# Where the split weights of a hybrid decoder block start in SBUF: six slots of 512-byte multiples

## The chip, the cores and the metric

The kernel runs on one core of one Trainium2 chip. The metric is the device time of one execution in microseconds (us); smaller is better. A difference of about 0.2% is what repeated timing of this kernel can tell from no change.

## The reference

One layer of a decoder block over 512 tokens of 2048 channels, in float32. Nearly all of its work is in dense products with weight matrices:

```python
mod = c_act @ w_ada[l] + b_ada[l]                      # 6 x 2048 modulation values
h = rmsnorm(x, norm_mix_g[l]) * (1.0 + sc_m) + sh_m
proj = h @ w_in[l]                                     # nine parts: conv, HGRN2, two gates
y_a = (a_b * causal_depthwise_conv(a_c * a_x, conv_w[l])) @ w_conv_out[l]
o = hgrn2_chunked(qh, kh, vh, log_f)                   # chunks of 64 tokens, 8 heads
y_b = o.reshape(b, s, D_HGRN_V).astype(x.dtype) @ w_hgrn_out[l]
merged = jax.nn.sigmoid(gate_a) * y_a + jax.nn.sigmoid(gate_b) * y_b
x = x + gt_m * (merged @ w_o[l])
h2 = rmsnorm(x, norm_ffn_g[l]) * (1.0 + sc_f) + sh_f
ff = (jax.nn.silu(h2 @ w_ffn_gate[l]) * (h2 @ w_ffn_up[l])) @ w_ffn_down[l]
return rmsnorm(x + gt_f * ff, norm_final_g)
```

## The kernel before, in words

Activations stand channel-major: 128 channels by 512 tokens. A product keeps float32 accuracy by splitting both operands into a high part, rounded to the reduced type `fp32r`, and a low part, the rest. It then needs three matmuls for each pair of blocks: high weights with high activations, high weights with low activations, low weights with high activations. `mm3` (lines 233 to 235), `v_block` (lines 351 to 353) and `m3` (lines 629 to 631) write out these three. Every matmul comes with its own load of a 128 by 128 block of weights, which the profile lists as engine PEld and which runs ahead of the matmul it belongs to.

Weights come by DMA as raw float32 tiles in the order of use. ScalarE casts a raw tile into `hi`, VectorE subtracts to get `lo` (lines 166 and 167 in `w_prep`; 674 to 684 in `quad_s` and `quad_c`; 1085 and 1086 in `u_prep`, where the tiles are called `uh` and `ul`). Each of the two names has a ring of three buffers, so weights are prepared up to two tiles ahead. `w_tile` makes a tile of the wanted size plus 32 elements, and starts the weights either at the beginning of the tile or, with `half`, 16 elements (64 bytes) into it.

Which weights take `half`:

- Without it: weights used with 512 columns of activations at once. These are the projections of the first and third stage (`proj`, `panel`, lines 233 to 235) and the down projection of the FFN (`down`, kind "D", lines 629 to 631). Also without it: the weights of `v_block`, where the activations are the loaded block and the weights are what streams through, 256 columns at a time.
- With it: weights used with 256 columns. These are the Strassen and plain passes of the gates and of the FFN (kinds "S" and "C", lines 629 to 631) and the token halves of the output projection.
- Kind "H" (eight tiles of the first FFN pass) is not in the ring: these weights stay for a second use in tiles of the pool `sactb`.

In time the program runs as follows. From 0 to about 157 us are the first norm, the modulation of the first norm on VectorE, and the first panels of `w_in`. Up to about 773 us come the rest of `w_in` and the HGRN2 core, the latter spread as background work. Up to about 1055 us are the gates (256 columns). Up to about 1400 us come the output projections of the two branches and `w_o`, beside which VectorE computes the other modulation values from 92 tiles of `w_ada` (line 311). The rest is the FFN, where the passes of 256 columns alternate with `down` (512 columns), and a tail.

The tiles are placed one behind the other in SBUF. In the first rings (pool `wts`) a tile takes 1056 elements, 4224 bytes, which is 8 times 512 plus 128; in the FFN's rings (pool `wts2`) it takes 928 elements, 3712 bytes, 7 times 512 plus 128. The first slot starts at a multiple of 512 bytes (117760 and 39936). So the six slots start 0, 128, 256 bytes (the three of `hi`) and 384, 0, 128 bytes (the three of `lo`) past a multiple of 512. A block of 128 weights is 512 bytes long, so every block in a tile has the offset of its tile. In use the slots follow each other as **A** (hi 0, lo 384), **B** (hi 256, lo 128), **C** (hi 128, lo 0), A, and so on.

Of the kernel before, what the change touches and what calls it, by code (L numbers as in the profile page):

```python
# [9 lines left out]
F32R = mybir.dt.float32r  # L10
# [4 lines left out]
P = 128  # L15
T = 512
D = 2048
# [25 lines left out]
WFULL = 5  # L43
HCB = 5
WOFF = 16

COL_C = 0
COL_B = 16
# [14 lines left out]
def hybrid_block_kernel(ctx: ExitStack, tc: tile.TileContext, xt, cols, crow, wam, war, wst, win, wco, who, wo, wgt, wg, wu, wd,  # L63
# [4 lines left out]
    def nm(s):  # L68
        cnt[0] += 1
        return f"{s}{cnt[0]}"  # L70
# [13 lines left out]
    wp = s1.enter_context(tc.tile_pool(name="wts", bufs=3, reuse_waits="tile"))  # L84
# [47 lines left out]
    def flat(t):  # L132
        return t.rearrange("p a b -> p (a b)")

    wlist = []
    wstate = {"dma": 0, "prep": 0, "use": 0, "raw": {}, "hl": {}, "half": ()}

    def w_tile(pool, shape, tag, name, half):
        a, b = shape[1:]
        t = pool.tile([P, a * b + 32], F32R, tag=tag, name=nm(name))  # L140
        o = WOFF if half else 0
        return t[:, o:o + a * b].rearrange("p (a b) -> p a b", b=b)

    def w_pair(shape, half=False):
        return [w_tile(wp, shape, t, t, half) for t in ("hi", "lo")]

    def w_dma():
        i = wstate["dma"]
# [8 lines left out]
    def w_prep():  # L157
        i = wstate["prep"]
        if i >= len(wlist):
            return  # L160
        while wstate["dma"] <= i:
            w_dma()
        raw = wstate["raw"].pop(i)
        hi, lo = w_pair((P, 4, 256), i in wstate["half"])
        nw = wlist[i].shape[-1]
        S.copy(flat(hi)[:, 0:nw], raw[:, 0:nw])  # L166
        V.tensor_tensor(flat(lo)[:, 0:nw], raw[:, 0:nw], flat(hi)[:, 0:nw].bitcast(F32), op=ALU.subtract)  # L167
        wstate["hl"][i] = (hi, lo)
        wstate["prep"] = i + 1

    def next_w(look=LOOK):
        i = wstate["use"]
        while wstate["prep"] <= min(i + look, len(wlist) - 1):
            w_prep()
        while wstate["dma"] <= min(i + look + 1, len(wlist) - 1):
            w_dma()
        wstate["use"] = i + 1
        return wstate["hl"].pop(i)
# [198 lines left out]
    for n in range(KC):  # L377
        g = n // 4
        w = [flat(t)[:, 0:512 if g else 768].rearrange("p (a b) -> p a b", b=256) for t in next_w(1)]
# [293 lines left out]
    def quad_s(sm, raw, hi, lo):  # L673
        S.copy(hi[:, 0:3, :], raw[:, 1:4, :])  # L674
        V.tensor_tensor(sm[:, 0:2, :], raw[:, 1:3, :], raw[:, 0:1, :].to_broadcast([P, 2, P]), op=ALU.subtract)
        V.tensor_tensor(sm[:, 2, :], sm[:, 1, :], raw[:, 1, :], op=ALU.add)
        V.tensor_tensor(sm[:, 3, :], raw[:, 3, :], sm[:, 2, :], op=ALU.subtract)  # L677
        S.copy(hi[:, 3:7, :], sm)  # L678
        V.tensor_tensor(lo[:, 0:3, :], raw[:, 1:4, :], hi[:, 0:3, :].bitcast(F32), op=ALU.subtract)
        V.tensor_tensor(lo[:, 3:7, :], sm, hi[:, 3:7, :].bitcast(F32), op=ALU.subtract)  # L680
# [85 lines left out]
    def g_prep():  # L766
        i = gs["prep"]
        while gs["dma"] <= i:
            g_dma()
        _, _, u, strassen = glist[i]  # L770
        raw = gs["raw"].pop(i)[:, u, :, :]
        hi, lo = w_pair((P, 8, P), True)
        if strassen:
            quad_s(gs["sm"](), raw, hi, lo)
        else:
            quad_c(raw, hi, lo)
        gs["hl"][i] = (hi, lo)
        gs["prep"] = i + 1
# [191 lines left out]
    torder = [(j, 0) for j in range(TU)] + [(j, 1) for j in range(TU)] + [(j, u) for j in range(TU, 8) for u in range(2)]  # L970
    ulist.extend((wd[j, 10], u, "D" if i < TU else "T") for i, (j, u) in enumerate(torder))
    kept = []
    us = {"dma": 0, "prep": 0, "use": 0, "raw": {}, "hl": {}, "pool": None, "after": ()}

    def u_dma():
        i = us["dma"]
        src = ulist[i][0] if i < tail0 else wd[(i - tail0) // 2, 10]
        raw = wr2.tile([P, 2, 4, P], F32, tag="raw", name=nm("ur"))
        nc.sync.dma_start(raw, src.rearrange("p (u b n) -> p u b n", u=2, b=4))
        if i < tail0:  # L980
            us["raw"][i] = us["raw"][i + 1] = raw
        else:
            for u in range(2):
                us["raw"][tail0 + torder.index(((i - tail0) // 2, u))] = raw
        us["dma"] = i + 2
# [77 lines left out]
    def u_prep():  # L1063
        i = us["prep"]
        while i not in us["raw"]:
            u_dma()
        _, u, kind = ulist[i]
        raw = us["raw"].pop(i)[:, u, :, :]
        pool = us["pool"] if kind == "T" else wp2
        shp = [P, 4, P] if kind == "T" else [P, 7, P]  # L1070
        if kind == "H":
            k = len(kept)
            t = sb[k // 2][k % 2]
            hi, lo = (t[:, 1 + 2 * b:3 + 2 * b, :].rearrange("p a (c n) -> p (a c) n", n=P) for b in range(2))
            kept.append((hi, lo))
        else:
            hi = w_tile(pool, shp, "hi", "uh", kind != "D")
            lo = w_tile(pool, shp, "lo", "ul", kind != "D")
        if kind == "S":
            quad_s(wp2.tile([P, 4, P], F32, tag="sm", name=nm("us"), bufs=2), raw, hi, lo)  # L1080
        else:
            with ExitStack() as order:
                for ins in us["after"] if i >= len(ulist) - 12 else ():
                    order.enter_context(tc.issue_after(ins.ins))
                S.copy(hi[:, 0:4, :], raw)  # L1085
                V.tensor_tensor(lo[:, 0:4, :], raw, hi[:, 0:4, :].bitcast(F32), op=ALU.subtract)  # L1086
        us["hl"][i] = (hi, lo)
        us["prep"] = i + 1

    def u_ahead(n=ULOOK):  # L1090
        i = us["use"]
        for k in range(i, min(i + n + 1, len(ulist))):
            if ulist[k][2] == "T" and us["pool"] is None:
                break
            if us["prep"] <= k:
                u_prep()
        while us["dma"] <= min(i + n + 3, len(ulist) - 2):
            u_dma()
# [206 lines left out]
    for tok in HALF:  # L1305
        outs = []
        for j in range(8):
# [12 lines left out]
            for e in range(2):  # L1320
                n = 2 * j + e
# [82 lines left out]
```

## Time and profile before

| | |
|---|---|
| median of 3 runs | 2822.83 us (2821.8 to 2823.86) |
| the profiled execution | 2818.55 us, span in the trace 2816.8 us |
| mean granted TensorE clock | 0.991 |
| VectorE, ScalarE busy | 2217.8 us (79%), 1100.1 us (39%) |
| DMA traffic | 414.23 MB, 147 GB/s on average |

In the rows that follow, a group of instructions is given as line, engine, operation, output and inputs by the program's names, partitions by elements, count, busy time in us, mean duration of one in ns, and what its engine waited for ahead of it. The recorded duration of a matmul is longer than the distance between the starts of two of them, because they are pipelined. The offsets of the weights are those of the section above; the trace names the tiles but not their addresses.

### The profile page before, as it was taken

What the parts mean: (1) busy time and instruction counts of PE and PEld (TensorE: products, weight loads), DVE (VectorE), ACT (ScalarE), POOL (GpSimd) and SP (SyncE); (2) the same over time, 40 slices, a digit from 0 to 9 for tenths busy, and PEclk for the clock granted to TensorE, in tenths of its full rate; (3) what the DMA queues carried; (4) which work ended last, traced back from release to release, by engine and by line L of the source; (5) the groups of instructions that cost most, each with busy time, mean ns of one, the idle gap of its engine ahead of it and who ended that gap; (6) DMA issues with size and microseconds to landing.
All of it is one profiled execution on the core that took longest, in us unless ns stands there. A gap on an engine that the chain in (4) does not pass through costs nothing.

```text
span 2816.8 us, 46688 instructions
## 1 busy us (share of the span) xinstructions
PE 2741.5 (97%) x18524; PEld 2461.4 (87%) x18524; DVE 2217.8 (79%) x4326; ACT 1100.1 (39%) x1723; POOL 1.3 (0%) x7
## 2 busy tenths in 40 slices
PE   5999999999999999899999999999999999999997
PEld 3788888888799997787899899998989989898997
DVE  7998963836799996786789787796968879687786
ACT  4333422323245552222375343343434334343445
POOL 0000000000000000000000000000000000000000
PEclk8999999999999999999999999999999999999999
DMA  9865632322233348898744333333333333333333
GB/s 351 302 215 187 207 100 83 97 91 90 76 101 118 124 148 298 294 315 287 239 143 127 100 112 101 109 106 98 113 99 112 99 104 113 98 113 98 105 106 105
DMA packets 117616, 414.23 MB, mean 147 GB/s; under 512 B 12818, under 2 KB 17170, under 8 KB 117396
## 3 DMA queue, kind: packets, MB, share of 16 engines
q1 hardware_dynamic: 116244, 407.04, 43.9%
q10 hardware_dynamic: 1152, 4.19, 0.4%
q8 instruction: 145, 2.38, 0.4%
q14 instruction: 75, 0.61, 0.1%
HBM read 398.59 MB, written 12.59 MB: 146 GB/s over the span
## 4 chain that ended last, share of the span: by engine, by line
PE 81%; DVE 8%; DMA 8%; issue 2%; ACT 1%; SPq 0%; DVEq 0%; ACTq 0%
PE st L631 18%; PE st L630 18%; PE st L629 18%; PE m L233 7%; PE m L235 7%; PE m L234 7%; DMA wm<-in_war_dram 6%; DVE o L311 2%; DVE wm L311 1%; DVE lo L167 1%; PE x L488 1%; PE m L353 1%; PE m L351 1%; PE m L352 1%; PE m L631 1%
## 5 line engine op out<-in xcount | busy, mean ns | idle before, releaser
L233 PE MATMUL m<-h,hi 128*128 128x512 f32 (+1 forms) x1152 | 436.0, 380 | 18.2 <-ACT hi L166 14.8
L631 PE MATMUL st<-sb,ul 128*128 128x256 f32 x1638 | 452.4, 276 | 0.3 <-DVE ul L680 0.3
L630 PE MATMUL st<-sb,uh 128*128 128x256 f32 x1638 | 452.3, 276 | 0.0
L629 PE MATMUL st<-sb,uh 128*128 128x256 f32 x1638 | 452.2, 276 | 0.0
L235 PE MATMUL m<-h,lo 128*128 128x512 f32 (+1 forms) x1152 | 437.0, 379 | 7.9 <-DVE lo L167 7.7
L234 PE MATMUL m<-h,hi 128*128 128x512 f32 (+1 forms) x1152 | 435.1, 378 | 0.3 <-DVE h L338 0.3
L166 ACT CAST hi<-wr 128x1024 fp32r<-128x1024 f32 (+2 forms) x199 | 201.7, 1017 | 532.9 <-PE m L234 381.7
L167 DVE TENSOR_TENSOR lo<-wr,hi 128x1024 fp32r<-128x1024 f32 (+2 forms) x199 | 234.8, 1182 | 118.1 <-ACT hi L166 116.9
L674 ACT CAST uh<-ur 128x384 fp32r<-128x384 f32 x326 | 167.3, 513 | 362.0 <-PE st L630 239.5
L631 PEld LDWEIGHTS st<-sb,ul 128*128 128x128 f32 x1638 | 307.6, 188 | 1.0 <-DVE ul L680 0.5
L629 PEld LDWEIGHTS st<-sb,uh 128*128 128x128 f32 x1638 | 307.5, 188 | 0.4
L630 PEld LDWEIGHTS st<-sb,uh 128*128 128x128 f32 x1638 | 307.5, 188 | 0.0
L233 PEld LDWEIGHTS m<-h,hi 128*128 128x128 f32 x1152 | 219.7, 191 | 62.5 <-ACT hi L166 15.9
L235 PEld LDWEIGHTS m<-h,lo 128*128 128x128 f32 x1152 | 217.6, 189 | 52.8 <-DVE lo L167 13.2
L629 PE MATMUL st<-hc,uh 128*128 128x512 f32 (+1 forms) x656 | 256.9, 392 | 2.9 <-ACT hc L1245 2.0
L631 PE MATMUL st<-hc,ul 128*128 128x512 f32 (+1 forms) x656 | 257.5, 395 | 0.0
L630 PE MATMUL st<-hc,uh 128*128 128x512 f32 x648 | 255.4, 394 | 0.0
L234 PEld LDWEIGHTS m<-h,hi 128*128 128x128 f32 x1152 | 218.0, 189 | 42.7 <-DVE h L338 1.1
L1086 DVE TENSOR_TENSOR ul<-ur,uh 128x512 fp32r<-128x512 f32 x210 | 143.2, 686 | 141.0 <-ACT uh L1085 140.9
L1085 ACT CAST uh<-ur 128x512 fp32r<-128x512 f32 x210 | 129.0, 620 | 314.0 <-PE st L630 294.2
L680 DVE TENSOR_TENSOR ul<-us,uh 128x512 fp32r<-128x512 f32 x326 | 223.0, 684 | 1.7 <-ACT uh L678 1.6
L678 ACT CAST uh<-us 128x512 fp32r<-128x512 f32 x326 | 201.5, 618 | 51.1 <-DVE us L677 50.3
(306 smaller groups left out, 6199.0 us busy)
## 6 DMA issues: line engine op xcount, KB each, us to landing
wm<-in_war_dram SPq DMA_DIRECT2D x128, 512.0 KB, 4.5
wr<-in_win_dram SPq DMA_DIRECT2D x107, 512.0 KB, 3.5
ur<-in_wg_dram SPq DMA_DIRECT2D x96, 512.0 KB, 3.5
ur<-in_wu_dram SPq DMA_DIRECT2D x88, 512.0 KB, 3.5
ur<-in_wd_dram SPq DMA_DIRECT2D x88, 512.0 KB, 3.5
o<-in_wam_dram SPq DMA_DIRECT2D x64, 512.0 KB, 6.5
wr<-in_wgt_dram SPq DMA_DIRECT2D x60, 512.0 KB, 3.6
wr<-in_wo_dram SPq DMA_DIRECT2D x44, 512.0 KB, 4.2
```

The source lines that it names most:

```text
L166: S.copy(flat(hi)[:, 0:nw], raw[:, 0:nw])
L167: V.tensor_tensor(flat(lo)[:, 0:nw], raw[:, 0:nw], flat(hi)[:, 0:nw].bitcast(F32), op=ALU.subtract)
L233: TE.matmul(ps, wh, ah, start=first, stop=False)
L234: TE.matmul(ps, wh, al, start=False, stop=False)
L235: TE.matmul(ps, wl, ah, start=False, stop=last)
L629: TE.matmul(ps, wh, ah, start=first, stop=False, skip_group_check=True)
L630: TE.matmul(ps, wh, al, start=False, stop=False, skip_group_check=True)
L631: return TE.matmul(ps, wl, ah, start=False, stop=last, skip_group_check=True)
L674: S.copy(hi[:, 0:3, :], raw[:, 1:4, :])
L678: S.copy(hi[:, 3:7, :], sm)
L680: V.tensor_tensor(lo[:, 3:7, :], sm, hi[:, 3:7, :].bitcast(F32), op=ALU.subtract)
L1086: V.tensor_tensor(lo[:, 0:4, :], raw, hi[:, 0:4, :].bitcast(F32), op=ALU.subtract)
```

## The change

The rings of three `hi` and three `lo` buffers become six tiles with names of their own (`hi0` to `hi2`, `lo0` to `lo2`), used in turn by a counter that runs through both stages. A tile takes 1152 elements (4608 bytes, 9 times 512) or, where no more than 896 elements are needed, 1024 (4096 bytes, 8 times 512). So all six slots start at a multiple of 512 bytes. Weights for 512 columns stand at the beginning of their slot. Weights for 256 columns stand 64, 192 or 320 bytes (`hi`) and 448, 64 or 192 bytes (`lo`) into it.

| offset past a multiple of 512 bytes | before | after |
|---|---|---|
| `hi`, weights for 512 columns and of `v_block` | 0, 128, 256 by slot | 0 |
| `lo`, the same | 384, 0, 128 by slot | 0 |
| `hi`, weights for 256 columns | 64, 192, 320 by slot | 64, 192, 320 by slot |
| `lo`, the same | 448, 64, 192 by slot | 448, 64, 192 by slot |
| activations `sb`, `hc` of the FFN, working tiles `b` | 256 | 0 |
| activations `h`, `o`, `sa` | 0 | 0 |
| kind "H" in `sactb` | 256 | 0 |

The last rows come from the rings growing by 2304 bytes for each partition in both stages: what lies behind them moves up by that much. The weights of the tail (`tailw`) keep their size of 544 elements and their 64 bytes.

The instructions, their order on every engine, their sizes and what each waits for are the same before and after, the DMA queues' too. Only the names `uh` and `ul` turn into `hi` and `lo`, and the lines move.

```diff
+WSIZE = 1152
...
+    us = {"pool": None}
+    wstate = {"dma": 0, "prep": 0, "use": 0, "raw": {}, "hl": {}, "half": (), "slot": -1}
+
+    def w_tiles(pool, shape, half):
         a, b = shape[1:]
-        t = pool.tile([P, a * b + 32], F32R, tag=tag, name=nm(name))
-        o = WOFF if half else 0
-        return t[:, o:o + a * b].rearrange("p (a b) -> p a b", b=b)
+        n = a * b
+        if pool is us["pool"]:
+            return [pool.tile([P, n + 2 * WOFF], F32R, tag=t, name=nm(t))[:, WOFF:WOFF + n].rearrange("p (a b) -> p a b", b=b)
+                    for t in ("hi", "lo")]
+        k = wstate["slot"] = (wstate["slot"] + 1) % 3
+        out_ = []
+        for i, t in enumerate(("hi", "lo")):
+            o = WOFF + 2 * WOFF * ((3 * i + k) % 4) if half else 0
+            w = pool.tile([P, WSIZE if n > 896 else 1024], F32R, tag=f"{t}{k}", name=nm(t), bufs=1)
+            out_.append(w[:, o:o + n].rearrange("p (a b) -> p a b", b=b))
+        return out_
...
-        return [w_tile(wp, shape, t, t, half) for t in ("hi", "lo")]
+        return w_tiles(wp, shape, half)
...
-            hi = w_tile(pool, shp, "hi", "uh", kind != "D")
-            lo = w_tile(pool, shp, "lo", "ul", kind != "D")
+            hi, lo = w_tiles(pool, shp, kind != "D")
```

More of the change, by code (lines that the diff above doesn't have):

```diff
@@ L135, in hybrid_block_kernel @@
     wlist = []
-    wstate = {"dma": 0, "prep": 0, "use": 0, "raw": {}, "hl": {}, "half": ()}
-    def w_tile(pool, shape, tag, name, half):
+    us = {"pool": None}
+    wstate = {"dma": 0, "prep": 0, "use": 0, "raw": {}, "hl": {}, "half": (), "slot": -1}
+    def w_tiles(pool, shape, half):
         a, b = shape[1:]
-        t = pool.tile([P, a * b + 32], F32R, tag=tag, name=nm(name))
-        o = WOFF if half else 0
-        return t[:, o:o + a * b].rearrange("p (a b) -> p a b", b=b)
+        n = a * b
[9 more added lines that the diff above has]
+        return out_
     def w_pair(shape, half=False):
-        return [w_tile(wp, shape, t, t, half) for t in ("hi", "lo")]
+        return w_tiles(wp, shape, half)
     def w_dma():
@@ L972, in hybrid_block_kernel @@
     kept = []
-    us = {"dma": 0, "prep": 0, "use": 0, "raw": {}, "hl": {}, "pool": None, "after": ()}
+    us.update({"dma": 0, "prep": 0, "use": 0, "raw": {}, "hl": {}, "pool": None, "after": ()})
     def u_dma():
```

## The prediction

> **What bounds the kernel now.** I read the page's busy times and its chain of work first, then the busy times by stage.
>
> ```profile
> span 2816.8 us, 46688 instructions
> PE 2741.5 (97%) x18524; PEld 2461.4 (87%) x18524; DVE 2217.8 (79%) x4326; ACT 1100.1 (39%) x1723; POOL 1.3 (0%) x7
> ...
> PE 81%; DVE 8%; DMA 8%; issue 2%; ACT 1%; SPq 0%; DVEq 0%; ACTq 0%
> ```
>
> TensorE holds 81% of the chain that ended last. The busy times by stage (stage in us, its length, then each engine's busy time) say where it does:
>
> ```profile
> 0.00:157.00 157.00, 118.46 (x511) 91.41 (x511) 137.58 (x248) 62.14 (x79) 1.34 (x7) 0.91 0.86 322
> 157.00:773.00 616.00, 614.42 (x3813) 509.57 (x3814) 423.70 (x579) 198.34 (x207) 0.00 (x0) 1.00 0.38 124
> 1055.00:1400.00 345.00, 331.37 (x1565) 272.34 (x1564) 249.62 (x329) 89.45 (x91) 0.00 (x0) 0.99 0.84 288
> 1550.00:2700.00 1150.00, 1149.18 (x8108) 1064.93 (x8107) 914.54 (x2058) 459.37 (x824) 0.00 (x0) 1.00 0.33 105
> ```
>
> From 157 to 773 us TensorE is busy 614.4 of 616 us, from 1550 to 2700 us 1149.2 of 1150 us: there the end moves with every ns of a matmul. Up to 157 us VectorE is the fuller engine (137.6 against 118.5 us). From 1055 to 1400 us the chain is elsewhere. Here it is for that stage alone, with VectorE's row:
>
> ```profile
> by line: DMA wm<-in_war_dram 48.0%; DVE wm L311 11.0%; issue 9.9%; DMA modrow<-c_scratch 6.9%; DVE lo L167 4.1%; PE m L235 3.0%; PE m L234 2.9%; PE m L233 2.8%; DVE o L218 1.8%; DMA b<-u_scratch 1.5%; DMA gc<-o_scratch 1.4%; DVE x L905 1.3%
> ...
> L311 DVE SCALAR_TENSOR_TENSOR wm<-wm,modrow 128x1024 f32<-128x1024 f32 x92 | 112.4, 1224 | 79.8 <-DMA wm<-in_war_dram 62.3 <-DMA modrow<-c_scratch 16.7
> ```
>
> The 92 tiles of modulation weights hold 48% of that chain by their DMA, and matmuls under 9%.
>
> **What the start of the weights costs now.** No instruction is added, removed or moved, so the whole question is whether one takes longer or shorter at another address. Three down-projection tiles that follow each other are slots A, B and C, 12 matmuls each. First the starts, then the groups by line of B alone and of C alone, then the last matmul of B and the last of C alone:
>
> ```profile
> 1559.76 0.40 PE L629 MATMUL st<-hc,uh 128*128 128x512 f32 x1
> ...
> 1562.54 0.39 PE L629 MATMUL st<-hc,uh 128*128 128x512 f32 x1
> ...
> 1565.32 0.40 PE L629 MATMUL st<-hc,uh 128*128 128x512 f32 x1
> ...
> 1568.13 0.39 PE L629 MATMUL st<-hc,uh 128*128 128x512 f32 x1
> ```
>
> ```profile
> L631 PE MATMUL st<-hc,ul 128*128 128x512 f32 x5 | 2.0, 398 | 0.0
> L630 PE MATMUL st<-hc,uh 128*128 128x512 f32 x4 | 1.6, 396 | 0.0
> L629 PE MATMUL st<-hc,uh 128*128 128x512 f32 x4 | 1.6, 389 | 0.0
> ```
>
> ```profile
> L631 PE MATMUL st<-hc,ul 128*128 128x512 f32 x5 | 2.0, 398 | 0.0
> L629 PE MATMUL st<-hc,uh 128*128 128x512 f32 x4 | 1.6, 396 | 0.0
> L630 PE MATMUL st<-hc,uh 128*128 128x512 f32 x4 | 1.6, 396 | 0.0
> ```
>
> ```profile
> L631 PE MATMUL st<-hc,ul 128*128 128x512 f32 x1 | 0.4, 404 | 0.0
> ...
> L631 PE MATMUL st<-hc,ul 128*128 128x512 f32 x1 | 0.4, 393 | 0.0
> ```
>
> The starts are 2.78, 2.78 and 2.81 us apart: 8.37 us for 36 matmuls, **232.5 ns** each. In B, 2.78 us for 12 is 231.7 ns, and the recorded durations average 394.3: a recorded duration is the distance to the next start plus 163 ns. While a matmul runs, the next one's weights are loaded. So a row says what a load at a given offset does to the matmul beside it:
>
> - B, line 629: weights at 256, then the same block again at 256: 389 - 163 = 226 ns. Slot A (offset 0) has the same 389.
> - C, line 629, weights at 128 and again at 128: 396, so 233 ns.
> - From `hi` to `lo` and back, offset changing by 128: 396 to 398, so 233 to 235 ns.
> - The last of B, 128 to the next tile's 128: 404, so 241 ns. The last of C, 0 to 0: 393, so 230 ns.
>
> The same shape on the same data thus costs 226 to 241 ns by offsets alone, and 226 only where two blocks that follow each other both stand at a multiple of 256. After the change every pair does, and all at 0.
>
> Does that hold when three in a row, and every load, are at equal offsets? No row of before has it for 512 columns. One has it for 256: kind "H", where both `hi` and `lo` stand at 256, beside the same pass with the 64-byte start:
>
> ```profile
> L629 PE MATMUL m<-sa,sb 128*128 128x256 f32 x8 | 2.3, 283 | 0.0
> L630 PE MATMUL m<-sa,sb 128*128 128x256 f32 x8 | 2.3, 283 | 0.0
> L631 PE MATMUL m<-sa,sb 128*128 128x256 f32 x8 | 2.3, 283 | 0.0
> ...
> L629 PE MATMUL m<-sa,uh 128*128 128x256 f32 x7 | 1.9, 277 | 0.0
> ```
>
> All three lines take 283 - 163 = 120 ns, against 113 to 114 with the 64-byte starts. That is 6 to 7 ns dearer, but it is one constant price on every line: equal offsets at a multiple of 256 settle and do not swing between 226 and 241 as the mixed ones do. The nearest row of 512 columns with a load that repeats its offset at a multiple of 256 is line 629 in A and B, 389. So I take **226.5 ns** for every matmul of 512 columns after the change. The bounds from rows are 226 (best seen) and 241 (the worst equal pair); that neither end has been seen as a steady run of 512 columns is why the rivals below get over a third of the chance.
>
> By the Trainium skill, "TensorE: Matmul & The Clock Gate", Part 2, Step-by-step, loading the next weights "doesn't steal SBUF read bandwidth from the running matmul", as PE has two independent read ports. By that rule the sum below would be 0. The trace disagrees for this kernel: 389 against 396 on one line, by the offset of the weights.
>
> **The sum.** The gain for each matmul is 232.5 - 226.5 = 6.0 ns. The counts, by stage (to 157 us, to 773, 1050 to 1400, from 1400):
>
> ```profile
> L233 PE MATMUL m<-h,hi 128*128 128x512 f32 x117 | 46.9, 414 | 18.2 <-ACT hi L166 14.8 <-ACT h L337 3.3
> ...
> L233 PE MATMUL m<-h,hi 128*128 128x512 f32 x676 | 269.9, 399 | 0.0
> ...
> L233 PE MATMUL m<-o,hi 128*128 128x512 f32 x256 | 100.6, 393 | 0.0
> L233 PE MATMUL m<-h,hi 128*128 128x512 f32 x160 | 63.2, 395 | 0.0
> ...
> L629 PE MATMUL st<-hc,uh 128*128 128x512 f32 x640 | 251.7, 393 | 0.8 <-DVE x L914 0.8
> ```
>
> Each stands for three lines.
>
> - 157 to 773 us: 676 x 3 x 6.0 = 12.2 us, all on the chain.
> - From 1400 us: 640 x 3 x 6.0 = 11.5 us, all on the chain.
> - 1055 to 1400 us: 416 x 3 x 6.0 = 7.5 us. The modulation DMAs stay as they are, and TensorE waits 13.6 us already; what it gains it mostly waits. Between 0 and 7.5 I take 1.5, a fifth, near the end that the chain's 48% of DMA points to.
> - To 157 us: 117 x 3 x 6.0 = 2.1 us beside a fuller VectorE. Between 0 and 2.1 I take 0.
>
> Against it stands `v_block`, whose streamed weights move to offset 0, the activations it loads being at 0 already:
>
> ```profile
> L353 PE MATMUL m<-lo,h 128*128 128x256 f32 x208 | 58.6, 282 | 1.6 <-DVE lo L167 1.6
> L352 PE MATMUL m<-hi,h 128*128 128x256 f32 x208 | 58.4, 281 | 0.0
> ```
>
> At kind "H"'s 283 it pays 1 to 2 ns, 624 x 1.5 = 0.9 us. Kind "H" itself goes from 256 to 0 with its activations; I take nothing for it, as A and B price 0 and 256 alike. Weights for 256 columns keep their offsets, so they keep their 276. VectorE and ScalarE write these slots too, and their price does not hang on the offset: VectorE's subtraction of 512 elements takes the same at odd multiples of 64 (line 680) as mostly at multiples of 128 (line 1086):
>
> ```profile
> L1086 DVE TENSOR_TENSOR ul<-ur,uh 128x512 fp32r<-128x512 f32 x210 | 143.2, 686 | 141.0 <-ACT uh L1085 140.9
> ...
> L680 DVE TENSOR_TENSOR ul<-us,uh 128x512 fp32r<-128x512 f32 x326 | 223.0, 684 | 1.7 <-ACT uh L678 1.6
> ```
>
> What hides next: from 157 to 773 us VectorE is busy 424 of 616 us and from 1550 us 915 of 1150, so neither takes over at 2% less. Sum: 12.2 + 11.5 + 1.5 - 0.9 = 24.3 us. The profiled execution, 2818.55 us, would become 2794.2; the median lies 4.3 us higher, so from 2822.83 I forecast **2799 us** (-0.86%). Its own range runs from everything gained (33.3 us, less 0.9: 2790) to 5.0 ns on the two bound stages alone (19.7 less 0.9: 2804).
>
> **The rivals.**
>
> 1. *Equal offsets settle higher.* The 226 needs a preceding change from `lo` back to `hi`; with every load at 0, each matmul costs what the last of C does, 230 ns. For it: that row, 0 to 0. Against: the next one at 0, line 629 of A, is 389 again. Gain 2.5 ns x 3948 = 9.9 us less 0.9: 2814. If two thirds of them stay at 233 and one third at 226, 230.8 on average, it is 2817.
> 2. *The loads collide more, and it is slower.* Spreading by 128 bytes let the weights slip past the stream; with all at one offset each load meets it as the last of B does. The place is lines 630 and 631, which now never see equal offsets except at tile ends. It decides from 232.5 ns on. At 241 ns each: 8.5 x 3948 = 33.6, and with a part of the DMA-bound stages (about 7) and `v_block` 2864 us. Milder, 7 ns over the forecast as kind "H" is over the 64-byte starts (233.5): 1.0 x 3948 = 3.9, plus 0.9 and 1 to 2 us of the other stages: 2829. For it: 404 and 393 on equal offsets. Against: 389, and kind "H"'s constant 283.
> 3. *Nothing happens*, because offsets only look like the cause (the lines also differ in which operand repeats): then 2823. Against: line 629 is 389 in B and 396 in C, with the same operands repeated.
> 4. *Equal offsets lose no time at all*, as the 64-byte starts nearly do: 220 ns, 12.5 x 3948 = 49 us, with the other stages 2770. No row of 512 columns is under 226.
>
> The Trainium skill's rule on the two read ports would give rival 3.
>
> **How the numbers follow.** Forecast 58%, rival 1 14%, rival 2 20% (233.5 ns 12%, 241 ns 8%), rival 3 4%, rival 4 4%. Within 0.2% means 2817 to 2828.5; less than that a measurement of this kernel can't tell. Faster: 58 + 4 + half of rival 1 = 69%. Slower: the 8, and two thirds of the 12: 16%. The same: 15%. The range leaves out rival 4 and the 241: from 2789 to 2831.
>
> **What would show it.** Right: line 629, 630 and 631 with 512 columns all at 389, a down tile 2.72 us long, TensorE's busy time in the FFN down by 11 us, the stage to 1400 us almost as long as now with more waits for line 311. Wrong: 630 or 631 at 396 or 404, or the 256-column groups off 276. If the 389s come and the time doesn't, look for waits of line 629 on VectorE that weren't there.

## The result and the profile after

| | before | after |
|---|---|---|
| median | 2823.03 us (6 runs, 2821.53 to 2823.89) | 2805.05 us (6 runs, 2801.43 to 2807.96) |
| the profiled execution | 2818.55 us, span 2816.8 | 2801.93 us, span 2800.2 |

The ratio is **0.9936**, 95% interval 0.9923 to 0.9949: 18 us less by the medians and 16.6 us by the two profiled executions. The forecast was 24 us less, 2799 us; 2805.05 lies 1 us above the range that the prediction gave this forecast (2790 to 2804).

First the busy times by stage of the changed kernel, in the columns used above:

```profile
0.00:157.00 157.00, 117.91 (x511) 91.60 (x511) 137.60 (x248) 62.10 (x79) 1.33 (x7) 0.90 0.86 322
157.00:773.00 616.00, 610.79 (x3834) 512.74 (x3834) 430.68 (x592) 201.84 (x210) 0.00 (x0) 1.00 0.39 125
...
1055.00:1400.00 345.00, 325.23 (x1554) 269.09 (x1553) 248.84 (x328) 88.90 (x89) 0.00 (x0) 0.99 0.83 286
...
1550.00:2700.00 1150.00, 1148.71 (x8187) 1071.19 (x8186) 922.10 (x2080) 463.87 (x834) 0.00 (x0) 1.00 0.34 106
```

In the same stretch from 157 to 773 us TensorE now gets 3834 matmuls done where it got 3813, from 1550 to 2700 us 8187 where it got 8108. From 1055 to 1400 us it gets fewer done (1554 against 1565), and is idle 19.8 us instead of 13.6. (These stretches have fixed borders in time, so after the change each holds a slightly later piece of the program; the table at the end of this section compares matmul by matmul.)

Then the three down tiles that the prediction took apart, by the starts of their first matmuls:

```profile
1553.43 0.40 PE L639 MATMUL st<-hc,hi 128*128 128x512 f32 x1
...
1556.17 0.39 PE L639 MATMUL st<-hc,hi 128*128 128x512 f32 x1
...
1558.89 0.39 PE L639 MATMUL st<-hc,hi 128*128 128x512 f32 x1
...
1561.61 0.39 PE L639 MATMUL st<-hc,hi 128*128 128x512 f32 x1
```

They are 2.74, 2.72 and 2.72 us apart where they were 2.78, 2.78 and 2.81: the second and the third take 226.7 ns for each matmul, just the forecast's price. The first tile is dearer: its first five starts, behind matmuls of 256 columns, are 228 to 236 ns apart, all later ones 226 or 227. The first start also says what has been gained by this point: 1559.76 - 1553.43 = 6.3 us.

The groups with 512 columns, from 1400 us on and from 157 to 773 us, and `v_block` in the latter (lines 10 higher than before):

```profile
L639 PE MATMUL st<-hc,hi 128*128 128x512 f32 x640 | 250.6, 392 | 1.3 <-DVE x L924 1.3
L640 PE MATMUL st<-hc,hi 128*128 128x512 f32 x640 | 249.5, 390 | 0.0
L641 PE MATMUL st<-hc,lo 128*128 128x512 f32 x640 | 247.4, 389 | 0.0
...
L243 PE MATMUL m<-h,hi 128*128 128x512 f32 x683 | 271.4, 397 | 0.0
L245 PE MATMUL m<-h,lo 128*128 128x512 f32 x684 | 266.9, 390 | 0.1
L244 PE MATMUL m<-h,hi 128*128 128x512 f32 x683 | 266.3, 390 | 0.0
L361 PE MATMUL m<-hi,h 128*128 128x256 f32 x208 | 60.5, 291 | 0.0
L363 PE MATMUL m<-lo,h 128*128 128x256 f32 x208 | 58.9, 283 | 2.3 <-DVE lo L177 2.3
L362 PE MATMUL m<-hi,h 128*128 128x256 f32 x208 | 58.9, 283 | 0.0
```

From 1400 us on all three lines of the split product are now nearly alike. Lines 243 and 361 are the first of their three, and some long records (44 above 470 ns on line 243) raise their means to 397 and 291 (before the change the same two lines had 399 and 289). Counting only starts less than 245 ns apart, lines 243 to 245 stand at 227.0, 227.1 and 227.7 ns. The other two lines of `v_block` stand at the 283 ns that the prediction gave it.

What TensorE waits for in the stage from 1040 to 1400 us (line waited at, engine and line waited for, us in total, times, longest), before and after:

```profile
PE m L235 <- DVE lo L167: 7.8, 10, 1.8
PE m L234 <- DVE o L218: 5.9, 1, 5.9
```

```profile
PE m L245 <- DVE lo L177: 14.5, 15, 2.0
PE m L244 <- DVE o L228: 5.2, 1, 5.2
```

The wait for the low weights has grown by 6.7 us. It is VectorE that comes late with them; from 1060 to 1380 us it waits 67.2 us for the DMA of the modulation tiles itself (62.3 before).

Every instruction stands in the same order in both traces, so each matmul's start can be compared with its own start before. What had been gained by then:

| at (us in before) | gained (us) | gained in between |
|---|---|---|
| 150 | 0.0 | |
| 773 | 7.5 | 7.5 |
| 1050 | 7.5 | 0.0 |
| 1400 | 6.3 | -1.2 |
| 1550 | 6.3 | 0.0 |
| 2700 | 15.3 | 9.0 |
| last matmul | 16.8 | 1.5 |

The -1.2 us comes from a single pair of traces. From the same first to the same last matmul, the stage from 1050 to 1400 us takes 350.1 us before and 351.3 us after. In the experiments below that leave the modulation work as it is, it takes 350.7 to 354.2 us where the 512-column matmuls keep their old price (three traces) and 351.3 to 355.2 us where they have the new one (four traces). So the stage shows no gain in any of them, and whether it loses a little is not shown. The waits of TensorE there do differ: 13.7 to 17.1 us at the old price, 19.3 to 22.7 us at the new one.

### The profile page after: what moved, and what is told of

It is laid out like the page before. It is cut to its first block, busy times and chain, and to the rows that moved or that the text cites. A ratio compares the mean times of both kernels' runs of the same rounds, so it can differ in the third digit from the quotient of the medians.

```text
span 2800.2 us, 46688 instructions
## 1 busy us (share of the span) xinstructions
PE 2716.5 (97%) x18524; PEld 2454.9 (88%) x18524; DVE 2216.4 (79%) x4326; ACT 1099.6 (39%) x1723; POOL 1.3 (0%) x7
## 3 DMA queue, kind: packets, MB, share of 16 engines
q10 hardware_dynamic: 1152, 4.19, 0.4%
## 4 chain that ended last, share of the span: by engine, by line
PE 79%; DVE 9%; DMA 9%; issue 2%; ACT 1%; SPq 0%; DVEq 0%; ACTq 0%
PE st L639 18%; PE st L641 18%; PE st L640 18%; DMA wm<-in_war_dram 7%; PE m L243 6%; PE m L245 6%; PE m L244 6%; DVE o L321 2%; DVE wm L321 2%; DVE lo L177 1%; PE x L498 1%; PE m L641 1%; PE m L363 1%; PE m L640 1%; PE m L639 1%
## 5 line engine op out<-in xcount | busy, mean ns | idle before, releaser
L641 PE MATMUL st<-sb,lo 128*128 128x256 f32 x1638 | 452.3, 276 | 0.3 <-DVE lo L690 0.3
L640 PE MATMUL st<-sb,hi 128*128 128x256 f32 x1638 | 452.2, 276 | 0.0
L639 PE MATMUL st<-sb,hi 128*128 128x256 f32 x1638 | 452.2, 276 | 0.0
L245 PE MATMUL m<-h,lo 128*128 128x512 f32 (+1 forms) x1152 | 430.4, 374 | 11.5 <-DVE lo L177 11.0
L684 ACT CAST hi<-ur 128x384 fp32r<-128x384 f32 x326 | 167.4, 514 | 360.3 <-PE st L640 238.0
L641 PEld LDWEIGHTS st<-sb,lo 128*128 128x128 f32 x1638 | 307.5, 188 | 0.9 <-DVE lo L690 0.5
L639 PEld LDWEIGHTS st<-sb,hi 128*128 128x128 f32 x1638 | 307.5, 188 | 0.4
L640 PEld LDWEIGHTS st<-sb,hi 128*128 128x128 f32 x1638 | 307.5, 188 | 0.0
L690 DVE TENSOR_TENSOR lo<-us,hi 128x512 fp32r<-128x512 f32 x434 | 296.9, 684 | 2.0 <-ACT hi L688 1.8
L688 ACT CAST hi<-us 128x512 fp32r<-128x512 f32 x434 | 268.2, 618 | 63.6 <-DVE us L687 62.8
L245 PEld LDWEIGHTS m<-h,lo 128*128 128x128 f32 x1152 | 217.3, 189 | 56.3 <-DVE lo L177 18.6
L639 PE MATMUL st<-hc,hi 128*128 128x512 f32 (+1 forms) x656 | 255.2, 389 | 3.3 <-ACT hc L1254 2.0
L641 PE MATMUL st<-hc,lo 128*128 128x512 f32 (+1 forms) x656 | 251.9, 386 | 0.0
L640 PE MATMUL st<-hc,hi 128*128 128x512 f32 x648 | 251.7, 388 | 0.0
```

The lines of the kernel that those rows point to most:

```text
L245: TE.matmul(ps, wl, ah, start=False, stop=last)
L639: TE.matmul(ps, wh, ah, start=first, stop=False, skip_group_check=True)
L640: TE.matmul(ps, wh, al, start=False, stop=False, skip_group_check=True)
L641: return TE.matmul(ps, wl, ah, start=False, stop=last, skip_group_check=True)
```

## The experiments

Four theories had to be told apart: that the offset of the weights from a multiple of 256 counts; that only a repeat of one offset counts, wherever it lies; that the ring's new size or the moved activations make the gain; and that the stage to 1400 us loses its gain to the modulation DMA. Times are medians beside runs of the kernel before on the same chip, where single runs scattered more (up to 2817 to 2832 us) than in the timing above.

### The new ring with the old offsets

```diff
-            o = WOFF + 2 * WOFF * ((3 * i + k) % 4) if half else 0
+            o = WOFF + 2 * WOFF * ((3 * i + k) % 4) if half else ((0, 64, 32), (96, 32, 0))[i][k]
```

> Six slots of 512-byte multiples as in the change, but weights for 512 columns at the offsets of before (hi 0, 256, 128 and lo 384, 128, 0 bytes by slot in the order of use). Theory (the offsets of the weights make the gain, not the new ring or the activations that moved by 2304 bytes): lines 639 to 641 with 512 columns back at about 392, 396 and 397 ns, the time back at that of before, 2823 us (2819 to 2826). Rival (the ring's size or the activations' new offset 0 makes it): the time stays at 2802 to 2808 us and the lines at 389.

2823.32 us (10 runs) against 2824.09; ratio 0.9996, 0.9986 to 1.0007. The groups with 512 columns from 1400 us:

```profile
L640 PE MATMUL st<-hc,hi 128*128 128x512 f32 x640 | 253.2, 396 | 0.0
L641 PE MATMUL st<-hc,lo 128*128 128x512 f32 x640 | 252.4, 397 | 0.0
L639 PE MATMUL st<-hc,hi 128*128 128x512 f32 x640 | 251.8, 393 | 0.0
```

These are before's 396, 397 and 393 again, with the activations where the change put them. The gain is the offsets' alone. The run also bears out the offsets that were worked out for before, which no trace shows: here they are written into the kernel, and the three lines come out the same.

### All at 256, all at 128, all at 64

The same line with 64, 32 or 16 elements in place of 0, that is 256, 128 or 64 bytes. It moves the streamed weights of `v_block` too, which are not in the rows shown:

```diff
-            o = WOFF + 2 * WOFF * ((3 * i + k) % 4) if half else 0
+            o = WOFF + 2 * WOFF * ((3 * i + k) % 4) if half else 64
...
+            o = WOFF + 2 * WOFF * ((3 * i + k) % 4) if half else 32
...
+            o = WOFF + 2 * WOFF * ((3 * i + k) % 4) if half else 16
```

> Weights for 512 columns, hi and lo of all slots, 256 bytes into their slot. Theory (a repeated offset at a multiple of 256 counts): 389 ns on all three lines and the time of the changed kernel, 2801 to 2808 us. Rival (only a start at a multiple of 512 is cheap): 396 or more, some 6 ns more on 3948 matmuls, 2825 us or more.

> Weights for 512 columns all 128 bytes into their slot, so every load repeats its offset, but not at a multiple of 256. Theory: slot C of before showed 396 ns for a repeated 128, and 404 at its first; so 233 to 241 ns each against 227: 2825 to 2860 us. Rival (equal offsets alone count, wherever they are): 389 ns and 2801 to 2808 us.

> Weights for 512 columns all 64 bytes into their slot, as those for 256 columns are. Theory (an odd multiple of 64 keeps the load out of the stream's way, as with 256 columns, where it costs 113 against 120 ns): one step of 6.7 ns less, 220 ns, 382 recorded, 2802 less 27, about 2778 us. Rival (with 512 columns another rule holds, since the load fills only the first half of the matmul): 389 ns or more, 2801 us or more.

All at 256: 2798.17 us, ratio 0.9906 (0.9886 to 0.9926). All at 128: 2824.96 us, 0.9997 (0.9984 to 1.0009). All at 64: 2826.43 us, 1.0000 (0.9985 to 1.0015). The same groups, in this order of the three kernels:

```profile
L639 PE MATMUL st<-hc,hi 128*128 128x512 f32 x640 | 250.5, 391 | 0.2 <-DVE x L924 0.2
L640 PE MATMUL st<-hc,hi 128*128 128x512 f32 x640 | 249.5, 390 | 0.0
L641 PE MATMUL st<-hc,lo 128*128 128x512 f32 x640 | 247.4, 389 | 0.0
```

```profile
L639 PE MATMUL st<-hc,hi 128*128 128x512 f32 x640 | 253.7, 396 | 0.9 <-DVE x L924 0.9
L640 PE MATMUL st<-hc,hi 128*128 128x512 f32 x640 | 252.6, 395 | 0.0
L641 PE MATMUL st<-hc,lo 128*128 128x512 f32 x640 | 250.9, 394 | 0.0
```

```profile
L639 PE MATMUL st<-hc,hi 128*128 128x512 f32 x640 | 254.1, 397 | 0.4 <-DVE x L924 0.4
L640 PE MATMUL st<-hc,hi 128*128 128x512 f32 x640 | 253.0, 395 | 0.0
L641 PE MATMUL st<-hc,lo 128*128 128x512 f32 x640 | 251.3, 395 | 0.0
```

256 does as well as 0. A repeated 128 or 64 is no better than the mixture of before, so a repeat alone is worth nothing. The theory's range for 128 was met at best at its lower edge: 232 ns on average where it had 233 to 241, with distances from 228 to 241 that follow each other in a repeating pattern. For 64 the theory was wrong: with 512 columns the start that serves 256 columns best is the worst of those tried, if only by 1 ns.

### hi at 0, lo at 256

```diff
-            o = WOFF + 2 * WOFF * ((3 * i + k) % 4) if half else 0
+            o = WOFF + 2 * WOFF * ((3 * i + k) % 4) if half else 64 * i
```

> Weights for 512 columns: hi at the beginning of its slot, lo 256 bytes into it, so that the offset changes at every step from hi to lo and back, but always by 256. Theory (the offset counts modulo 256 bytes, and no repeat is needed): 389 ns on all three lines, the time of the changed kernel, 2798 to 2808 us. Rival (what costs in before is the change of offset itself, whatever its size): lines 640 and 641 at 396 as in slots A and B, some 2815 us or more.

2804.83 us, ratio 0.9945 (0.9930 to 0.9959), and the groups at 392, 390 and 389 ns. The offset counts modulo 256; nothing has to repeat.

### The activations moved along

`hs` gives the high and low FFN activations tiles of 1088 elements and starts them 32 elements in; the down weights (tiles of at most 896 elements) start 32 elements in as well.

```diff
+            o = WOFF + 2 * WOFF * ((3 * i + k) % 4) if half else 32 if n <= 896 else 0
...
+    def hs():
+        return hcp.tile([P, 1088], F32R, tag="hc", name=nm("hc"))[:, 32:1056].rearrange("p (a b) -> p a b", b=T)
...
-        hi, lo = hc(F32R), hc(F32R)
+        hi, lo = hs(), hs()
```

> The changed kernel, but in the down projection of the FFN (1920 matmuls of 512 columns, lines 641 and ahead) both the weights and the activations hc stand 128 bytes past a multiple of 256. Theory (what counts is the offset of the weights from that of the streamed activations, modulo 256): 389 ns on all three lines as in the changed kernel. Rival (the weights' own address counts): about 395 ns as in the run with all weights at 128, some 10 us more.

One run: 2805.8 us, and

```profile
L639 PE MATMUL st<-hc,hi 128*128 128x512 f32 x640 | 250.4, 391 | 0.3 <-DVE x L924 0.3
L640 PE MATMUL st<-hc,hi 128*128 128x512 f32 x640 | 249.1, 389 | 0.0
L641 PE MATMUL st<-hc,lo 128*128 128x512 f32 x640 | 247.5, 389 | 0.0
```

Weights at 128 cost 394 to 396 against activations at 0, and 389 to 391 against activations at 128. For 512 columns, what counts is the distance between the two operands, modulo 256 bytes. For 256 columns the same run speaks against so simple a rule: most matmuls of the tail that stream `hc` are 117 to 119 ns apart where the changed kernel has 113 or 114, though, as far as the kernel's text tells, weights and activations there still stand an odd multiple of 64 bytes apart. The addresses in the tail are not on record, and this stays open.

### v_block's streamed weights at 64

The weights of `v_block`, which stream while activations are loaded, get the starts of the other weights for 256 columns; `vhalf` collects their places in the list.

```diff
+    vhalf = wstate["half"] = set()
...
+            if panels[g][n % 4] == 20:
+                vhalf.add(len(wlist))
...
+            vhalf.update(range(len(wlist) - 4, len(wlist)))
```

> The changed kernel with the streamed weights of v_block (lines 361 to 363, 768 matmuls of 256 columns) at the starts 64 to 448 bytes, as the other weights for 256 columns. Theory (for 256 columns an odd multiple of 64 between loaded block and stream takes 113 instead of 120 ns, whichever of the two is the weights): lines 361 to 363 at 276 ns instead of 283 in the stage from 157 to 773 us, 624 x 7 ns = 4.4 us less. Rival (only the loaded block's offset counts, and that stays at 0): 283 ns and no gain.

2802.99 us, ratio 0.9927 (0.9909 to 0.9945), not to be told from the change itself. The forecast of 113 ns failed (these are lines 368 to 370 of this kernel): over the 595 undisturbed matmuls of the stage to 773 us a `v_block` matmul gained 2.1 ns on the changed kernel, 1.3 us in all, and most starts are 117 or 118 ns apart, not 120 and not 113. A few that wait hide even this in the group means. Why the exchanged roles do not reach 113 stays open.

### Half of each modulation tile left out, with the old and the new offsets

These two kernels load and multiply only half the columns of each of the 128 later modulation tiles, 92 of them in the stage from 1050 to 1400 us and 36 ahead of it. So both the DMA and VectorE's multiplication (line 311, or 321) are halved.

```diff
-                    nc.sync.dma_start(flat(wt), war[md * KC + n, half])
-                    mod_dot(wt, mstate["row"], mpart[:, KC * half + n:KC * half + n + 1])
+                    nc.sync.dma_start(wt[:, 0, :], war[md * KC + n, half][:, 0:T])
+                    mod_dot(wt[:, 0:1, :], mstate["row"][:, 0:1, :], mpart[:, KC * half + n:KC * half + n + 1])
```

> The kernel before, with half the columns of each later modulation tile loaded and multiplied (128 tiles, lines 311 and below): a part of the modulation is left out. Theory (from 1055 to 1400 us the DMA of these tiles sets the pace): the waits of TensorE there (13.6 us in before) mostly go; about 2808 to 2814 us. Rival (the pace there is TensorE's own): no change, 2819 us or more.

> The changed kernel with the same half of the modulation tiles left out. Theory (what the change gains on the 1248 matmuls from 1055 to 1400 us is waited away for the modulation DMA): with that DMA halved the stage keeps its gain of about 6 us, so this run is 23 to 25 us below the run of the kernel before with the same part left out, where the change as it stands gained 17 to 18. Rival (the gain is lost there for another reason): 17 to 18 us here too.

Old offsets: 2800.03 us. New offsets: 2780.40 us, 19.6 us less; between the two profiled executions (2799.45, and 2776.79, the fastest of its four) it is 22.7 us. Against before's runs the medians are at 0.9925 and 0.9854. From the same first to the same last matmul the stage from 1050 to 1400 us takes 336.2 us with the old offsets and 329.8 us with the new ones: 6.4 us less, where the change as it stands gained nothing. The chain in that stage, in the changed kernel first, then with the halved tiles:

```profile
by line: DMA wm<-in_war_dram 49.9%; DVE wm L321 12.1%; issue 8.6%; DMA modrow<-c_scratch 6.3%; PE m L245 4.1%; PE m L243 3.9%; PE m L244 3.9%; DVE lo L177 3.9%; DVE x L915 1.3%; DVE b L914 1.3%; DVE x L924 1.2%; DVE x L900 1.0%; DVE o L228 
```

```profile
by line: PE m L245 27.6%; PE m L244 27.4%; PE m L243 27.4%; DMA wm<-in_war_dram 7.0%; PE st L641 2.0%; PE st L640 2.0%; PE st L639 2.0%; DVE wm L321 1.5%; DVE lo L177 1.4%; issue 0.9%; DVE x L900 0.3%; ACT hi L176 0.3%; DVE gc L672 0.2%; DV
```

The chain goes from the DMA to the three matmul lines, and with it the gain appears. By the traces the theory holds, for the modulation tiles as a whole: the chain had 50% on their DMA and 12% on VectorE's work on them, but the two were not halved apart. The difference of the medians, 19.6, falls between the two expectations. The forecast for the old offsets, 2808 to 2814, was too timid: the stage became 13.9 us shorter, of which the waits of TensorE (13.7 us before, 3.9 here) explain 9.8, and another 4.6 us had been gained by its start.

### A version below both

If these tiles are the limit, it helps to send for them earlier, where the DMA engines are busy 39% of the time. The budgets of the background work decide that; both versions have `v_block`'s weights at 64 as above.

```diff
-CORE_BUDGET = 1.0
+CORE_BUDGET = 1.5
...
-DVE_BUDGET = 3.0
+DVE_BUDGET = 4.0
```

> The changed kernel with v_block's weights at 64 bytes and the budget for modulation work in the stage to 773 us raised from 3.0 to 3.5, which moves 24 of the 92 later modulation tiles ahead of the gates. Theory (from 1055 to 1400 us their DMA sets the pace and swallows the change's gain there): that stage gives 6 to 15 us, the stage to 773 us loses little as VectorE has room (431 of 616 us), total 2788 to 2798 us, below both kernels. Rival (VectorE gets too full where the HGRN2 core runs): the stage to 773 us loses what the other gains, 2800 us or more.

> The same with budgets of 4.0 and, in the last head pair, 1.5: 53 of the 92 tiles move ahead of the gates. Theory: as the run with half of every tile left out, nearly all waits from 1055 to 1400 us go, some 15 to 20 us, and the earlier stage loses 0 to 10: 2782 to 2795 us. Rival: VectorE at about 495 of 616 us delays the low weights and the core, 2800 us or more.

With 24 tiles moved (budgets 3.5 and 1.0): 2797.23 us, ratio 0.9909 (0.9894 to 0.9924), an interval that still touches the change's own (0.9923 to 0.9949). With 53 moved, as in the diff: **2789.34 us**, ratio **0.9877** (0.9861 to 0.9894). The stages of the latter:

```profile
157.00:773.00 616.00, 610.81 (x3839) 512.16 (x3838) 492.63 (x698) 202.11 (x210) 0.00 (x0) 1.00 0.53 173
...
1055.00:1400.00 345.00, 333.62 (x1655) 280.43 (x1654) 194.96 (x227) 94.74 (x93) 0.00 (x0) 1.00 0.62 208
```

VectorE carries 62 us more up to 773 us and TensorE gets as many matmuls done there as in the changed kernel (3839 against 3834). From 1055 to 1400 us it gets 101 more done. Between the same two matmuls that stage takes 339.9 us where the changed kernel takes 351.3. TensorE's waits there are down to 11.4 us from 19.7, so not nearly all of them went, as the expectation had it; the total lies in the expected range all the same.

## Why the prediction came out as it did

- **That offsets decide, and that 226 to 227 ns would become the steady price**: right, on all three lines. The step from two rows (line 629 at a repeated multiple of 256, and kind "H") to a run that had not been seen held. The reason given was half right: the repeat does not matter, the distance between weights and stream modulo 256 does. In before that distance was 0 for `hi` of slots A and B, and for `lo` of C only. Kind "H" stood for a steady price, and that held; which way the price goes it could not say, as with 256 columns the distance of 0 is the dear one.
- **The mis-sized term is the gain for each matmul, 232.5 - 226.5 = 6.0 ns.** It measured 4.8 to 4.9 over the undisturbed matmuls, and 5.0 by the groups from 1400 us (393, 396, 397 before, 392, 390, 389 after). Both ends were off. The 232.5 came from a single round of A, B, C whose first tile is not yet settled (line 629 has 392 on average in that A, not the 389 that the prediction gives it), while all matmuls from 1400 to 2700 us average 232.1 and those from 157 to 773 us 231.7. And after, 8 to 10% still take 230 to 236, so that the mean is 227.0 to 227.2 and not 226.5. Over the undisturbed matmuls that makes some 9.3 us in each of the two bound stages, 18.6 instead of 23.7. So the measured time came out just above the forecast's own range, whose upper end stood for 5.0 ns in these two stages.
- **157 to 773 us**: 7.5 us instead of 12.2 less 0.9. Beside the smaller gain, `v_block` took 1.1 us in its steady matmuls and 0.7 at waits, twice its term.
- **1055 to 1400 us**: -1.2 instead of +1.5. That the modulation tiles would eat the gain was right, shown by the halved tiles and by the waits of all traces. The undisturbed matmuls there gained 5.8 us and the waits took 7.1. That a fifth of the gain remains shows in no trace, but this stage scatters by some 4 us at equal offsets, which is more than the term.
- **To 157 us** nothing, as forecast. **From 1400 us** 9.0 us up to 2700 us instead of 11.5; the last 1.5 us fell in the tail, mostly at waits, and were not forecast; in the other traces the tail moves by -2.5 to +1.5 us against before, whatever the offsets.
- **Rival 1** (230 ns) and **rival 2** (collisions at one offset) did not come; what rival 2 describes is what all at 128 or 64 do, at 232 to 233 ns on average, not at 241. (In rival 1, two thirds at 233 and one third at 226 make 230.7 ns, not 230.8; the time it gives stays the same.) **Rival 4** has no offset among those tried. **Rival 3** fell with the result, and with the run of old offsets, which brings the old time back. It is what would follow from the two independent read ports in the Trainium skill's "TensorE: Matmul & The Clock Gate", Part 2, Step-by-step; 389 against 395 ns on line 641, with all weights at 0 or all at 64 and nothing else changed, does not fit it, and the measurement decides.

## What to carry to other kernels

When a matmul-bound kernel's durations fall into groups on one line, compare the addresses of its two operands, not only of one. In this kernel the weights of a 512-column matmul in `fp32r` should start at the same place modulo 256 bytes as the streamed activations, and rings whose slots are not a multiple of 256 bytes spoil that silently. Count such a gain only over the stages whose chain is TensorE's, and take the price before from the group over all tiles, not from one round of them.

## What the runs showed of the hardware that was not expected

- The distance between weights and streamed operand modulo 256 bytes sets the pace of 512-column matmuls: 227 ns at 0, 232 on average at 128, 233 at 64. With 256 columns it is the other way about, 113 with the weights at odd multiples of 64 and the activations at 0, against 120 at distance 0; but with the roles exchanged, and in the tail of the run with the activations moved along, it is 117 to 119.
- Away from 0 the time from one start to the next does not settle at one value: at 128 it repeats a pattern between 228 and 241 ns, at 64 it alternates between 230 or 231 and 236.
- At a low granted clock none of this shows: from 36 to 40 us of before, where it is 0.51, the starts of the 512-column matmuls are 426 to 427 ns apart on all three lines, with `hi` and with `lo` weights alike. From 40 to 44 us, at a clock of 1.00, they are 224 to 238 ns apart.
- Runs of kernels with the same 227 ns scatter by 7 to 14 us (2801 to 2808, 2797 to 2805, 2803 to 2810, 2796 to 2810), and those with the halved tiles by 2 to 6. The stage from 1050 to 1400 us alone differs by up to 3.9 us between their traces; why stays open.
